# Attention's end in a hybrid backbone: the sixth head's norm in three groups, the last output products dealt differently, and a product and some low parts moved to VectorE

## The chip, the cores and the metric

One core of one Trainium2 chip runs the kernel. The metric is the device time of one execution in microseconds (us), and lower is better. Five engines work side by side, each on its own list of instructions in order: TensorE (PE, and PEld for its weight loads), VectorE (DVE), ScalarE (ACT), GpSimd (POOL) and SyncE (SP), whose list issues the DMAs. Semaphores make one engine wait for another.

## The reference

Two layers run over 1024 latent tokens and 256 context tokens of width 1024. The first layer mixes tokens by differential attention, the second by an S5 state-space layer; each is followed by a squared-ReLU MLP, and each sublayer has an RMS norm before and after it with a modulated scale, shift and gate. What the change touches is the end of the first mixer and the step from it to the MLP:

```
def attend(q, k, v):
    s = jnp.einsum('bqhcd,bkhcd->bhcqk', q, k).astype(jnp.float32)
    p = jax.nn.softmax(s, axis=-1)
    w = p[:, :, 0] - lam * p[:, :, 1]
    o = jnp.einsum('bhqk,bkhe->bqhe', w.astype(v.dtype), v)
    return rmsnorm(o, subln_g) * (1.0 - lambda_init)
...
y_lat = jnp.einsum('bte,ed->btd', o_l, w_o)
...
x = x + g1 * rmsnorm(y_lat, norm_g[i, 1])
h = rmsnorm(x, norm_g[i, 2]) * (1.0 + s2) + sh2
x = x + g2 * rmsnorm(sqrelu_mlp(h, mlp_w1[i], mlp_w2[i]), norm_g[i, 3])
```

There are 8 heads, so o has 8 slices of 128 columns per token (counted 0 to 7 here), and each is normed by itself before the product with w_o.

## The kernel before

**Numbers.** Every large product is made of three matmuls on numbers cut in a high and a low part (`mm3`, lines 132 to 134): high by high, high by low, low by high. `split` (lines 137 and 138) makes the parts: ACT copies the high part, then DVE, or POOL where it is named, subtracts it from the source to give the low part. So each cut is an ACT instruction and then one on DVE or POOL that waits for it.

**Attention** (`phase_b`) is written out by hand: inside `manual()` all engines but SP take their instructions in the order of the code. A step n handles unit u of head h (n = 9 h + u, 72 of them, then five closing steps 72 to 76). Unit 0 is the context's two query tiles, units 1 to 8 are one tile of 128 queries each. In a step PE makes the scores of its unit; DVE reads them out of PSUM with their maxima (line 592), ACT takes the two exponentials (602), DVE combines them (610 to 613). PE transposes the weights of the unit before in three parts (625): w0 (four 128-wide transposes), w1 (two) and w2 (four). w0 and w1 or w2 leave PSUM either directly (`w_direct`: ACT 631, then DVE 632) or through a copy (`w_copy`: ACT 638 and 641, then POOL 642). Every second step PE multiplies the weights by the values (`values`), and ACT takes the pair's output out of PSUM (732) and squares it (735); a later step has PE sum the squares (`pair_sums`, 740) into two PSUM columns.

PE's waits in a step are filled with products dealt to three places, `fill(0)` to `fill(2)`. From n = 63 on these are products of heads 0 to 5 with the left half of w_o for one token tile (`wo_group`, at the steps of `wo_at`); the tuple `a` says how many of the four or six products go to each place. Their sum leaves by ACT (858) and a DMA to `wod`. Heads 6 and 7 are added at the end: `wo_last` in steps 74 and 75 for tiles 8, 9 and 0 to 4, and in `phase_c` for tiles 5 to 7.

Head 6's norm happens while head 7 runs. For a pair of query tiles `load6` brings its output and its factors from DRAM in two buffers each, and `norm6` multiplies them on POOL (796) and splits the result, with the low part on POOL, into oT[..][:, 6]. At n = 69 and 70 two pairs each are loaded at the step's start and normed at its end, at n = 71 the fifth. Head 7's norm (`norm7`) is a step behind its sums: POOL writes a diagonal matrix (144, 811), PE multiplies it by ones so that the factors lie along columns (815), DVE applies them (817) and `split` cuts.

**The next stage** (`phase_c`, and `second_group` and `mlp0_head` behind it) is not ordered by hand: a scheduler sets each engine's order from the code. DVE adds head 6 and 7's part to the sum read back from DRAM (1486); then the right half of w_o is multiplied in the groups g = 2 (context, tiles 8 and 9), 0 (tiles 0 to 3) and 1 (tiles 4 to 7). For each tile `finish` runs a chain: ACT squares both halves with their sums (1438, 1439), DVE multiplies the right half by the gate row G (1440, reads PSUM), POOL multiplies the left half a by G (1443) and makes the factor (1441, 144), DVE scales and adds x (1447), ACT and POOL take the second norm (149, 150, 144), ACT scales (1454). When a group's tiles are done, `feature` (`to_feature`) turns them over: per k of 8, PE transposes (333) into one of two PSUM banks, DVE (338, even k) or ACT (336, odd k) applies scale and shift into one of two buffers, and `split` cuts the result, the low part on POOL for groups 2 and 0. The MLP's first products for the context and for group 0 (written H,RT in the views) follow on PE between these transposes.

Of the kernel before, what the change touches and what calls it, by code (L numbers as in the profile page):

```python
# [10 lines left out]
ALU = mybir.AluOpType  # L11
# [59 lines left out]
class Prog:  # L71
# [610 lines left out]
    def phase_b(self):  # L682
# [24 lines left out]
        pb = self.bank(6)  # L707
# [29 lines left out]
        def pair_sums(h, pair):  # L737
            b = pb[:, 0:2] if pair == 4 or h == 7 and pair > 2 else self.PS[:, 1790:1792]
            for i in range(2):
                mm(b[:, i : i + 1], sq[:, 128 * i : 128 * i + 128], self.ones, start=True, stop=True)  # L740
            nc.scalar.activation(hst[:, 1, h, 2 * pair : 2 * pair + 2], b, AF.Copy)
# [43 lines left out]
        buf6 = [(nob, nrb), (self.wv(6, 256), self.wv(7, 256))]  # L785
        pairs6 = {6: (0, 1), 7: (2, 3), 8: (4,)}

        def load6(u):
            for (ob, rb), pair in zip(buf6, pairs6[u]):
                self.dma(ob, self.od[6, :, 256 * pair : 256 * pair + 256])  # L790
                self.dma(rb, self.rsd[6, 2 * pair : 2 * pair + 2].rearrange("a b -> (a b)").partition_broadcast(128))

        def norm6(u):
            for (ob, rb), pair in zip(buf6, pairs6[u]):
                g, c0 = cols7[pair]
                nc.gpsimd.tensor_tensor(ob, ob, rb, ALU.mult)
                self.split(self.oT[g][0][:, 6, c0 : c0 + 256], self.oT[g][1][:, 6, c0 : c0 + 256], ob, nc.gpsimd)
# [90 lines left out]
        with self.manual():  # L888
            for n in range(72 + 5):
# [6 lines left out]
                if front and n - 6 >= 9 and (n - 6) % 9 < 5 and (n - 6) // 9 < 7:  # L896
                    norm_load((n - 6) // 9 - 1, (n - 6) % 9)
                if h == 7 and u > 5:
                    load6(u)
                if front:  # L900
# [16 lines left out]
                if groups:  # L917
                    if n < 63 or 0 < u < 3:
                        a = self.FILLS.get(u, (0, 1, 5, 8))
                    else:  # L920
                        a = (0, 4, 4, 4) if u == 0 else (0, 2, 5, 6) if late else (0, 2, 4, 6)
                    if n > 71:
                        a = (0, 2, 4, 6) if n == 72 else (0, 4, 6, 6)
                    fills = [groups[0][0][a[i] : a[i + 1]] for i in range(3)]
# [159 lines left out]
                if h == 7:  # L1084
                    beside7(u)
                    if u > 5:
                        norm6(u)
                if tail and tail[0][0] == n:
# [327 lines left out]
    def phase_c(self):  # L1416
# [13 lines left out]
        def finish(g, i, y):  # L1430
# [4 lines left out]
            def s0():  # L1435
                self.tile_dma(x0, i, x)
                st = self.stat.next()
                nc.scalar.activation(b, y, AF.Square, scale=1.0 / 32, accum_out=st[:, 1:2])
                nc.scalar.activation(b, a, AF.Square, scale=1.0 / 32, accum_out=st[:, 0:1])
                nc.vector.tensor_tensor(b, y, G[m][:, 512:1024], ALU.mult)  # L1440
                nc.gpsimd.tensor_scalar(st[:, 0:1], st[:, 0:1], st[:, 1:2], EPS, ALU.add, ALU.add)
                self.rsqrt(st[:, 2:3], st[:, 0:1])
                nc.gpsimd.tensor_tensor(a, a, G[m][:, 0:512], ALU.mult)
                r[0] = st[:, 2:3]
# [13 lines left out]
        def feature(g, k, tmps=tmps):  # L1458
            m = 1 if g == 2 else 0
            return self.to_feature([t[i] for i in self.G_TILES[g]], A[:, m], B[:, m], self.hT[g][0], self.hT[g][1],  # L1460
                                   tb, tmps, k, nc.vector if g == 1 and k % 2 else None, k % 2 == 1)

# [5 lines left out]
        for nb in range(2):  # L1468
            wt = [] if nb else [None] * 6
            for kk in range(0 if nb else 3, 4):  # L1470
                raw, hi, lo = raws.pop(0) if raws else self.wo_load(kk, nb), wr.next(), wr.next()
                for j in range(2):
                    self.split(hi[:, j], lo[:, j], raw[:, j])
                    wt.append((hi[:, j], lo[:, j]))
# [1204 lines left out]
```

## Time and profile before

| what | value |
|---|---|
| median of 3 runs | 2810.94 us |
| lowest and highest of them | 2810.39 and 2814.80 us |
| the profiled execution's own time | 2805.7 us |
| its span, first to last instruction | 2803.9 us |
| TensorE clock granted, mean of the span | 0.994 |
| PE / PEld / DVE busy | 2702.6 / 2251.9 / 2000.8 us |
| ACT / POOL busy | 1420.8 / 900.0 us |

Busy times are sums over the span. In a row of the timeline stand the start, the time from start to end, the engine, the line, what is written and read, how many instructions were merged, and in brackets how long the engine sat idle before and what ended that. A row of the windows gives a stretch, its length, the busy time of PE, PEld, DVE, ACT and POOL with their instruction counts, the clock granted to TensorE as a share of full speed, the share of the DMA engines that was busy, and GB/s. A PE matmul of 512 columns shows 0.39 us from start to end, but the next one starts 0.23 us after it, so PE's own lost time is better read from the starts and from the idle time of PEld, whose load begins each matmul.

### The profile page before, as it was taken

The numbers are of one execution on the slowest core, as the hardware profiler recorded it, in microseconds if no ns is written. First come the engines' busy times: TensorE is split into PE (matmuls) and PEld (weight loads), VectorE is DVE, ScalarE is ACT, GpSimd is POOL, SyncE is SP. The second block draws the span as 40 slices with busy tenths as digits, with TensorE's granted clock in tenths as the row PEclk, the third lists the DMA queues.
The fourth block names the chain that finished last, engine by engine and source line by source line (L and its number), as shares of the span: only waits on it lengthen the run. The fifth ranks groups of instructions, "written<-read, shape, count | busy, mean of one in ns | idle before, by whom it ended". The sixth has DMA issues, their size and how long they took to land. (4 is left out here: it accounts for less than half of the span.)

```text
span 2803.9 us, 43710 instructions
## 1 busy us (share of the span) xinstructions
PE 2702.6 (96%) x15645; PEld 2251.9 (80%) x15645; DVE 2000.8 (71%) x2994; ACT 1420.8 (51%) x2717; POOL 900.0 (32%) x729
## 2 busy tenths in 40 slices
PE   6999999999999999999999999799999999999999
PEld 4687888888777888888877788788787778888887
DVE  6366888888744777666898876899433687767566
ACT  3425677777655643333444444587344533345443
POOL 3312345554445400000120032687023053335414
PEclk9999999999999999999999999899999999999999
DMA  9944133333526378985899875689642254476544
GB/s 269 324 165 158 59 95 94 96 97 115 190 65 199 113 256 287 322 294 180 309 311 300 273 233 201 218 242 310 210 143 91 68 186 157 151 259 212 170 128 143
DMA packets 377448, 539.13 MB, mean 192 GB/s; under 512 B 38286, under 2 KB 231052, under 8 KB 374028
## 3 DMA queue, kind: packets, MB, share of 16 engines
q1 hardware_dynamic: 377228, 536.32, 58.6%
q8 instruction: 123, 2.02, 0.3%
q14 instruction: 97, 0.79, 0.1%
HBM read 367.54 MB, written 164.47 MB: 190 GB/s over the span
## 5 line engine op out<-in xcount | busy, mean ns | idle before, releaser
L132 PE MATMUL PS<-H 128*128 128x512 f32 x1072 | 420.5, 393 | 2.5 <-ACT H L137 1.4
L134 PE MATMUL PS<-H 128*128 128x512 f32 x1072 | 417.6, 390 | 3.2 <-DVE H L138 1.8
L133 PE MATMUL PS<-H 128*128 128x512 f32 x1072 | 417.7, 390 | 0.0
L132 PE MATMUL PS<-H,R 128*128 128x512 f32 (+1 forms) x828 | 307.8, 374 | 4.0 <-ACT R L137 1.5
L134 PE MATMUL PS<-H,R 128*128 128x512 f32 (+1 forms) x828 | 297.8, 360 | 0.9 <-POOL R L138 0.9
L133 PE MATMUL PS<-H,R 128*128 128x512 f32 (+1 forms) x828 | 298.1, 360 | 0.0
L132 PEld LDWEIGHTS PS<-H 128*128 128x128 f32 x1072 | 201.2, 188 | 50.4 <-issue 6.2
L134 PEld LDWEIGHTS PS<-H 128*128 128x128 f32 x1072 | 201.2, 188 | 46.6 <-DVE H L138 3.1
L133 PEld LDWEIGHTS PS<-H 128*128 128x128 f32 x1072 | 201.3, 188 | 40.6
L137 ACT ACTIVATE H<-U 128x640 fp32r<-128x640 f32 x216 | 131.9, 674 | 171.9 <-PE PS L133 143.9
L137 ACT ACTIVATE R<-W 128x512 fp32r<-128x512 f32 (+1 forms) x185 | 129.6, 707 | 171.4 <-PE PS L133 113.5
L132 PE MATMUL PS<-R,H 128*128 128x512 f32 x534 | 212.9, 400 | 3.2 <-ACT H L137 3.2
L134 PE MATMUL PS<-R,H 128*128 128x512 f32 x534 | 210.5, 395 | 1.8 <-DVE H L138 1.8
L133 PE MATMUL PS<-R,H 128*128 128x512 f32 x534 | 209.5, 393 | 0.0
L602 ACT ACTIVATE F<-F,stat 128x1280 f32<-128x1280 f32 x128 | 174.1, 1361 | 64.3 <-DVE F L592 64.3
L138 DVE TENSOR_TENSOR H<-U,H 128x640 fp32r<-128x640 f32 x216 | 167.0, 807 | 48.7 <-ACT H L137 45.5
L137 ACT ACTIVATE H<-W 128x512 fp32r<-128x512 f32 (+2 forms) x158 | 95.6, 614 | 198.4 <-PE PS L133 113.9
L138 DVE TENSOR_TENSOR H<-W,H 128x512 fp32r<-128x512 f32 (+1 forms) x137 | 125.9, 929 | 96.4 <-ACT H L137 95.9
L592 DVE TENSOR_SCALAR_CACHE_REDUCE F<-PS 128x1280 f32<-128x1280 f32 x128 | 185.3, 1485 | 13.0 <-PE PS L579 12.6
L642 POOL TENSOR_TENSOR R<-F,R 128x512 fp32r<-128x512 f32 (+1 forms) x88 | 119.3, 1367 | 209.9 <-ACT R L641 144.9
L132 PEld LDWEIGHTS PS<-H,R 128*128 128x128 f32 x828 | 156.9, 190 | 33.4 <-issue 4.1
L134 PEld LDWEIGHTS PS<-H,R 128*128 128x128 f32 x828 | 156.7, 189 | 26.4 <-POOL R L138 1.1
(529 smaller groups left out, 6688.4 us busy)
## 6 DMA issues: line engine op xcount, KB each, us to landing
W<-in_mlp_w SPq DMA_DIRECT2D x176, 256.0 KB, 3.7
U<-Aa SPq DMA_DIRECT2D x108, 320.0 KB, 4.4
Aa<-FU SPq DMA_DIRECT2D x91, 320.0 KB, 4.8
Ad<-F SPq DMA_DIRECT2D x112, 256.0 KB, 3.0
W<-Ad SPq DMA_DIRECT2D x112, 256.0 KB, 2.9
FU<-in_mlp_w SPq DMA_DIRECT2D x32, 512.0 KB, 5.9
Ta<-FU SPq DMA_DIRECT2D x16, 1024.0 KB
U<-in_ada_w SPq DMA_DIRECT2D x32, 512.0 KB, 9.1
```

The source lines that it names most:

```text
L132: mm(out, ah, bh, start=first, stop=False, **kw)
L133: mm(out, ah, bl, start=False, stop=False, **kw)
L134: mm(out, al, bh, start=False, stop=last, **kw)
L137: self.nc.scalar.activation(hi, src, AF.Copy)
L138: (lo_eng or self.nc.vector).tensor_tensor(lo, src, hi.bitcast(F32), ALU.subtract)
L592: ts(p[c], self.PS[:, 1792 * c : 1792 * c + 1280], 1.0, None, ALU.mult, ALU.min, accum_out=sm[:, c : c + 1])
L602: nc.scalar.activation(p[c], p[c], AF.Exp, bias=sm[:, c : c + 1], scale=-1.0, accum_out=sn[:, 0:1] if c else s0[:, u + 1 : u + 2])
L642: self.nc.gpsimd.tensor_tensor(lo, t, hi.bitcast(F32), ALU.subtract)
```

## The change

Six edits. (1) Head 6's norm runs in three groups, a step apart each: products on POOL (`norm6`) at the ends of steps 69, 71 and 73, the splits (`halves6`) at the ends of 70, 72 and 74; the next group's loads follow the splits. (2) At n = 63 one product moves from `fill(0)` to `fill(2)`; in the late steps 69 and 71 one moves from `fill(2)` to `fill(1)`. (3) The sums of head 7's last two pairs go to PSUM bank 5 in place of bank 6, which also holds the transposed weights and the last values. (4) a*G goes from POOL to DVE. (5) Group 0's low parts go from POOL to DVE. (6) One low part of w_o's last rows goes from DVE to POOL.

```
-            b = pb[:, 0:2] if pair == 4 or h == 7 and pair > 2 else self.PS[:, 1790:1792]
+            b = self.bank(5)[:, 0:2] if h == 7 and pair > 2 else pb[:, 0:2] if pair == 4 else self.PS[:, 1790:1792]
...
-        def norm6(u):
-            for (ob, rb), pair in zip(buf6, pairs6[u]):
+        def norm6(j):
+            for ob, rb in buf6[: len(pairs6[j])]:
+                nc.gpsimd.tensor_tensor(ob, ob, rb, ALU.mult)
+
+        def halves6(j):
+            for (ob, rb), pair in zip(buf6, pairs6[j]):
                 g, c0 = cols7[pair]
-                nc.gpsimd.tensor_tensor(ob, ob, rb, ALU.mult)
                 self.split(self.oT[g][0][:, 6, c0 : c0 + 256], self.oT[g][1][:, 6, c0 : c0 + 256], ob, nc.gpsimd)
...
-                if h == 7 and u > 5:
-                    load6(u)
+                if n == 69:
+                    load6(0)
...
-                        a = (0, 4, 4, 4) if u == 0 else (0, 2, 5, 6) if late else (0, 2, 4, 6)
+                        a = (0, 3, 3, 4) if u == 0 else (0, 2, 6, 6) if late else (0, 2, 4, 6)
...
-                    if u > 5:
-                        norm6(u)
+                if n in (69, 71, 73):
+                    norm6((n - 69) // 2)
+                if n in (70, 72, 74):
+                    halves6((n - 70) // 2)
+                    if n < 74:
+                        load6((n - 68) // 2)
...
-                nc.gpsimd.tensor_tensor(a, a, G[m][:, 0:512], ALU.mult)
+                nc.vector.tensor_tensor(a, a, G[m][:, 0:512], ALU.mult)
...
-                                   tb, tmps, k, nc.vector if g == 1 and k % 2 else None, k % 2 == 1)
+                                   tb, tmps, k, nc.vector if g == 0 or g == 1 and k % 2 else None, k % 2 == 1)
...
-                    self.split(hi[:, j], lo[:, j], raw[:, j])
+                    self.split(hi[:, j], lo[:, j], raw[:, j], None if nb or j else nc.gpsimd)
```

The lines of the new kernel stand 3 to 7 higher: 811 is 814 there, 815 is 818, 858 is 861, 1440 is 1447, 1443 is 1450, 1447 is 1454.

ACT's order before, from the end of step 69 to the exponentials of step 71 (H<-W is head 6's high part, FC head 7's output, 631 step 70's w0):

```order
L858 ACTIVATE W<-PS 128x512
L137 ACTIVATE H<-W 128x256 x2
L631 ACTIVATE R_110<-PS 128x4x128
L602 ACTIVATE F_1851,FC<-F_1851,stat 128x1280
L602 ACTIVATE F_1851,stat<-F_1851,stat 128x1280
L638 ACTIVATE F_1851<-PS 128x512
L631 ACTIVATE R_110<-PS 128x2x128
L641 ACTIVATE R_110<-F_1851 128x4x128
L741 ACTIVATE FC<-PS 128x2
L858 ACTIVATE W<-PS 128x512
L137 ACTIVATE H<-FC 128x256
L137 ACTIVATE H<-W 128x256 x2
```

And the same stretch now:

```order
L861 ACTIVATE W<-PS 128x512
L631 ACTIVATE R_110<-PS 128x4x128
L602 ACTIVATE F_1851,FC<-F_1851,stat 128x1280
L602 ACTIVATE F_1851,stat<-F_1851,stat 128x1280
L638 ACTIVATE F_1851<-PS 128x512
L631 ACTIVATE R_110<-PS 128x2x128
L641 ACTIVATE R_110<-F_1851 128x4x128
L741 ACTIVATE FC<-PS 128x2
L861 ACTIVATE W<-PS 128x512
L137 ACTIVATE H<-FC 128x256
L137 ACTIVATE H<-W 128x256 x2
```

The first two copies of head 6 have left the place ahead of step 70's w0; those that stand at the end of step 70 are now of the first group, whose products POOL made a step earlier.

POOL's order now, over the same steps and on to the diagonals of step 73 (795 is head 6's product, R_110<-W the split of w_o's last rows, 814 a diagonal):

```order
L795 TENSOR_TENSOR W<-W 128x256 x2
L642 TENSOR_TENSOR R_110<-F_1851,R_110 128x4x128
L138 TENSOR_TENSOR H<-FC,H 128x256
L138 TENSOR_TENSOR R_110<-W,R_110 128x1024
L138 TENSOR_TENSOR H<-W,H 128x256 x2
L144 TENSOR_TENSOR FC<-FC,mhalf 128x2
L814 TENSOR_SCALAR FC<-ident,FC 128x128 x2
```

These rows begin at the end of step 71: two products stand there where one product and its low part stood, and two low parts now stand between the split of w_o and the diagonal that PE waits for in step 73.

DVE's order before, for the chains of tiles 5 and 6 and the first features of group 0 (FA<-PS,FB is the right half by G, 1447 the scaling with x added, 338 a feature's scale and shift):

```order
L1440 TENSOR_TENSOR FA<-PS,FB 128x512
L1447 SCALAR_TENSOR_TENSOR W<-FA,stat,W 128x1024
L338 TENSOR_SCALAR FA<-PS,modc 128x512
L1440 TENSOR_TENSOR FA<-PS,FB 128x512
L1447 SCALAR_TENSOR_TENSOR W<-FA,stat,W 128x1024
L338 TENSOR_SCALAR FA<-PS,modc 128x512
```

And now:

```order
L1447 TENSOR_TENSOR FA<-PS,FB 128x512
L1450 TENSOR_TENSOR FA<-FA,FB 128x512
L1454 SCALAR_TENSOR_TENSOR W<-FA,stat,W 128x1024
L338 TENSOR_SCALAR FA<-PS,modc 128x512
L1447 TENSOR_TENSOR FA<-PS,FB 128x512
L1450 TENSOR_TENSOR FA<-FA,FB 128x512
L1454 SCALAR_TENSOR_TENSOR W<-FA,stat,W 128x1024
L138 TENSOR_TENSOR H<-FA,H 128x512 x2
L338 TENSOR_SCALAR FA<-PS,modc 128x512
L138 TENSOR_TENSOR H<-FA,H 128x512
```

A product (1450) has come between each tile's 1447 and its scaling, and group 0's low parts (138, H<-FA) stand between the features' 338. Over the program DVE has 17 instructions more (10 products, 8 low parts, one low part less) and POOL 17 fewer; all differences of order lie between step 63 and the MLP's first products.

More of the change, by code (lines that the diff above doesn't have):

```diff
@@ L785, in phase_b, with load6 @@
         buf6 = [(nob, nrb), (self.wv(6, 256), self.wv(7, 256))]
-        pairs6 = {6: (0, 1), 7: (2, 3), 8: (4,)}
-        def load6(u):
-            for (ob, rb), pair in zip(buf6, pairs6[u]):
+        pairs6 = (0, 1), (2, 3), (4,)
+        def load6(j):
+            for (ob, rb), pair in zip(buf6, pairs6[j]):
                 self.dma(ob, self.od[6, :, 256 * pair : 256 * pair + 256])
                 self.dma(rb, self.rsd[6, 2 * pair : 2 * pair + 2].rearrange("a b -> (a b)").partition_broadcast(128))
-        def norm6(u):
-            for (ob, rb), pair in zip(buf6, pairs6[u]):
+        def norm6(j):
+            for ob, rb in buf6[: len(pairs6[j])]:
+                nc.gpsimd.tensor_tensor(ob, ob, rb, ALU.mult)
+        def halves6(j):
+            for (ob, rb), pair in zip(buf6, pairs6[j]):
                 g, c0 = cols7[pair]
-                nc.gpsimd.tensor_tensor(ob, ob, rb, ALU.mult)
                 self.split(self.oT[g][0][:, 6, c0 : c0 + 256], self.oT[g][1][:, 6, c0 : c0 + 256], ob, nc.gpsimd)
```

## Prediction

> **What bounds the kernel now.** I read the page first:
>
> ```profile
> span 2803.9 us, 43710 instructions
> PE 2702.6 (96%) x15645; PEld 2251.9 (80%) x15645; DVE 2000.8 (71%) x2994; ACT 1420.8 (51%) x2717; POOL 900.0 (32%) x729
> ```
>
> TensorE is busy 96% of the span, so a change of order can only win back what TensorE loses. Two windows, both far behind the edited stretch, show what follows it:
>
> ```profile
> 1050.00:1100.00 50.00, 50.00 (x270) 39.98 (x270) 37.03 (x60) 17.36 (x34) 0.00 (x0) 1.00 0.89 307
> 1770.00:1775.00 5.00, 0.37 (x2) 0.37 (x2) 4.14 (x4) 3.47 (x7) 1.72 (x5) 0.66 1.05 340
> ```
>
> In the MLP TensorE has no gap at all (50.00 of 50), so an earlier start there is an earlier end; at 1770, in the S5 stage, it stands still (0.37 of 5) while the DMA engines are full. Then I took the edited stretch, 735 to 945 us, and listed what TensorE's loads waited for. First how a wait is read, from the end of step 72:
>
> ```profile
> 822.69 0.39 PE L133 MATMUL PS<-R,H 128*128 128x512 f32 x1
> 822.92 0.40 PE L134 MATMUL PS<-R,H 128*128 128x512 f32 x1
> 823.94 0.52 PEld L740 LDWEIGHTS PS<-lamc,adat 128*128 128x128 f32 x4 [1.05 <-DVE R L632]
> ```
>
> Matmuls start 0.23 apart, so the one at 822.92 held TensorE until 823.15, and the sums of squares started at 823.94: 0.79 was lost where the load shows 1.05 idle. About 0.26 of such an idle time is no loss, and I take it off below.
>
> The largest wait of the attention's end is in step 70, with the rows of all engines in order of time:
>
> ```profile
> 797.90 0.60 PE L625 MATMUL PS<-ident,F 128*128 128x128 f32 x4
> 798.01 1.49 DVE L592 TENSOR_SCALAR_CACHE_REDUCE F<-PS 128x1280 f32<-128x1280 f32 x1
> 798.71 0.42 ACT L137 ACTIVATE H<-W 128x256 fp32r<-128x256 f32 x1 [3.09 <-POOL W L796]
> 799.21 0.74 POOL L138 TENSOR_TENSOR H<-W,H 128x256 fp32r<-128x256 f32 x1 [0.53 <-ACT H L137]
> 800.67 0.42 ACT L137 ACTIVATE H<-W 128x256 fp32r<-128x256 f32 x1 [1.53 <-POOL W L796]
> 800.99 0.58 ACT L631 ACTIVATE R<-PS 128x512 fp32r<-128x512 f32 x1
> 801.60 0.69 DVE L632 TENSOR_TENSOR R<-PS,R 128x512 fp32r<-128x512 f32 x1 [2.10 <-ACT R L631]
> 802.35 0.20 PEld L625 LDWEIGHTS PS<-ident,F 128*128 128x128 f32 x2 [2.28 <-DVE R L632]
> 804.79 0.52 PEld L740 LDWEIGHTS PS<-lamc,adat 128*128 128x128 f32 x4 [1.03 <-ACT F L638]
> ```
>
> w0's transposes end at 798.50, but ACT sits in front of head 6's first high part until POOL's product is there (3.09), then of the second (1.53), and copies w0 only at 800.99. VectorE's low part follows at 801.60 and w1's transposes, which need its bank, at 802.35: TensorE waited 2.28. The other waits, of steps 63, 71 and 74:
>
> ```profile
> 738.36 0.52 PEld L740 LDWEIGHTS PS<-lamc,adat 128*128 128x128 f32 x4 [1.52 <-ACT F L638]
> 816.71 0.42 PEld L625 LDWEIGHTS PS<-ident,F 128*128 128x128 f32 x4 [1.36 <-DVE R L632]
> 833.77 0.52 PEld L740 LDWEIGHTS PS<-lamc,adat 128*128 128x128 f32 x4 [0.91 <-DVE FC L817]
> ```
>
> and behind them those before the last rows of w_o and in the next stage, with the clock there:
>
> ```profile
> 846.67 0.53 PEld L132 LDWEIGHTS PS<-RT,H 128*128 128x128 f32 x3 [1.20 <-ACT RT L137]
> 848.06 3.69 DVE L138 TENSOR_TENSOR RT<-W,RT 128x512 fp32r<-128x512 f32 x6
> 848.80 0.19 PEld L133 LDWEIGHTS PS<-RT,H 128*128 128x128 f32 x1 [1.60 <-DVE RT L138]
> ```
>
> ```profile
> 874.72 0.20 PEld L333 LDWEIGHTS PS<-ident,FB 128*128 128x128 f32 x2 [0.86 <-ACT FB L1454]
> 884.71 0.20 PEld L333 LDWEIGHTS PS<-ident,FB 128*128 128x128 f32 x2 [0.53 <-DVE FA L338]
> 890.63 0.20 PEld L333 LDWEIGHTS PS<-ident,FB 128*128 128x128 f32 x2 [1.11 <-ACT FA L336]
> 913.68 0.42 PEld L333 LDWEIGHTS PS<-ident,FB 128*128 128x128 f32 x4 [2.74 <-DVE FA L338]
> 915.42 0.71 PEld L333 LDWEIGHTS PS<-ident,FB 128*128 128x128 f32 x4 [0.58 <-ACT FA L336]
> 920.40 0.42 PEld L333 LDWEIGHTS PS<-ident,FB 128*128 128x128 f32 x4 [1.24 <-DVE FA L338]
> ```
>
> ```profile
> 910.00:915.00 5.00, 2.68 (x15) 1.85 (x13) 2.27 (x3) 2.94 (x8) 2.33 (x4) 0.98 0.58 207
> 915.00:920.00 5.00, 4.28 (x23) 3.73 (x21) 3.10 (x3) 2.80 (x5) 4.82 (x6) 0.68 0.37 106
> ```
>
> The features' transposes wait for the banks that VectorE (338) and ScalarE (336) empty, and behind the longest gap, 2.74, the granted clock falls to 0.68 for a window.
>
> **The change part by part.** *Step 63.* One product leaves the place ahead of w0, so w0 and all behind it come its 0.68 (3 x 0.23) earlier, and it runs again inside the 1.52 that TensorE waited for the copy of w2. Gain 0.68; the cover is the 1.52, and were it gone the gain would be nil.
>
> *Step 70.* The product-and-split pairs become two products alone, with the ACT copies a step later. ACT is then free when w0 is there. What is late next is VectorE: its second maxima end at 798.01 + 1.49 = 799.50, so the low part moves from 801.60 to 799.50, and w1's transposes, 0.75 behind it, to 800.25, where TensorE arrives anyway. The sums at 804.79 hang on ACT's two exponentials and copy behind w0; ACT starts these about 2.4 earlier (798.60 for 800.99), so I take 2.4 for the step, 2.0 at the least (2.28 less 0.26), 3.0 at most (with all of the 1.03).
>
> *Step 71.* The ACT copies at its start no longer wait for POOL, and a fourth product fills the place ahead of w2's transposes. That wait was 1.36, a loss of 1.1; filled by 0.68 and shortened by the earlier ACT, I take all of it: 1.1 (0.7 by the product alone).
>
> *Steps 72 and 74.* In bank 5 the sums wait neither for w0's low part nor for head 7's multiplication (817), which were the releasers: 0.79 and 0.91 - 0.26 = 0.65. Both go unless the next matmul then waits (below). The DMAs of head 6 are issued later, behind the splits of the group before; no product to DRAM is held by them for longer than before, since the waiting buffer is free one POOL instruction after ACT's copy. Attention's end together: 0.68 + 2.4 + 1.1 + 0.79 + 0.65 = 5.6.
>
> *Last rows of w_o.* The first low part goes to POOL, which is idle there, in 1.29 (the row of a 128x512 low part below); on VectorE it stood behind the sums that wait for DRAM, until 848.06. ACT's high part is there when the first matmul that reads it starts, 846.67, so the low part ends by 847.9 in place of 848.06 + 0.62 = 848.7: 0.8 of the 1.60. Bounds nil and 1.34.
>
> *The product a*G.* The chain of one tile before:
>
> ```profile
> 909.31 0.69 DVE L1440 TENSOR_TENSOR FA<-PS,FB 128x512 f32<-128x512 f32 x1 [2.55 <-ACT FA L1439]
> 909.76 1.30 POOL L1443 TENSOR_TENSOR FA<-FA,FB 128x512 f32<-128x512 f32 x1
> 911.01 0.58 POOL L144 TENSOR_TENSOR stat<-stat,mhalf 128x1 f32<-128x1 f32 x1
> 911.62 1.28 DVE L1447 SCALAR_TENSOR_TENSOR W<-FA,stat,W 128x1024 f32<-128x1024 f32 x1 [1.62 <-POOL stat L144]
> 912.83 0.81 DVE L338 TENSOR_SCALAR FA<-PS,modc 128x512 f32<-128x512 f32 x1
> ```
>
> POOL's product (1.30) stands between the sum's first step and the root at 911.01, which releases the scaling at 911.62 and so the feature at 912.83. Without it the root comes 1.25 earlier; on VectorE the same product takes about 0.69 (the 1440 row, the same shape from PSUM) in the time in which VectorE waits for the root (1.62). So each of ten chains becomes some 1.25 shorter, and 0.69 is hidden in the wait that remains.
>
> *Group 0's low parts.* Eight of them leave POOL and go to VectorE:
>
> ```profile
> 921.98 1.29 POOL L138 TENSOR_TENSOR H<-FA,H 128x512 fp32r<-128x512 f32 x1 [0.26 <-ACT H L137]
> 935.52 1.67 DVE L1512 TENSOR_TENSOR FA<-FA,H 128x512 f32<-128x512 f32 x1
> ```
>
> At 921.98 one took 1.29 on POOL. On VectorE a low part of this shape takes 3.69 / 6 = 0.62 when it runs alone (the row at 848.06), and an operation with the same shape and both inputs in SBUF took 1.67 at 935.52, when POOL ran a low part beside it. These are the bounds, 8 x 0.62 = 5.0 and 8 x 1.67 = 13.4; POOL is left with little but roots in this stretch, so I take the lower end, and add the delay it makes where it stands between features.
>
> The Trainium skill's SBUF page (SBUF — State Buffer, "Who interferes with whom") says that a VectorE instruction with two SBUF inputs and a GpSimd instruction that reads SBUF exclude each other for a whole instruction; the 1.67 here agrees. By that rule the moved work gains only where POOL is quiet.
>
> What TensorE gets of it: the waits at 874.72, 884.71 and 890.63 (0.86 + 0.53 + 1.11, less 3 x 0.26 = 1.7) are chains of groups 2 and 0, each shorter by more than its wait; I take 1.7. The next, 2.74 and 0.58, end at tile 5's chain, in front of which tile 4's stands in the same queues: two times 1.25 cover 2.48 (2.74 - 0.26), and the 0.58 is the odd feature behind the same. The 1.24 at 920.40 stands behind tile 6's chain, and here two low parts now stand in VectorE's order ahead of the feature. I take 2.74 + 0.58 + 1.24 - 0.78 = 3.8 less 1.0 that stays, 2.8; bounds 0 and 3.8. And the clock: 5 x 0.32 + 5 x 0.02 = 1.7 us of work lost in the two windows. It fell right behind the 2.74 and not behind the 2.28 of step 70, so with that gap gone I count all 1.7.
>
> The Trainium skill's page TensorE: Matmul & The Clock Gate ("What's actually happening") lets the clock fall only after an idle window of about 3.4 us, longer than this gap; by that rule the gap was not the cause, the 1.7 would stay, and the gain would be 1.7 smaller. The trace here shows the fall behind 2.74, and I go by it.
>
> Sum: 5.6 + 0.8 + 1.7 + 2.8 + 1.7 = 12.6 us. The profiled execution took 2805.7 (span 2803.9) and would take 2793.1; it lies 5.2 below the median of the runs, 2810.94, from which I take the same 12.6: 2798.3.
>
> **The rivals.** *The rest does not follow.* TensorE comes 12.6 earlier into an MLP where the DMA engines are 0.89 busy, and into the S5 stage, where TensorE stands while they are full. If the loads there keep their own time, the gain is swallowed: 2810.9. Against it: TensorE shows no wait on a load in the MLP, and the loads are issued as their buffers come free, so earlier too.
>
> *POOL becomes late in step 73.* There head 7's factors need POOL's diagonal:
>
> ```profile
> 830.18 0.72 POOL L811 TENSOR_SCALAR FC<-ident,FC 128x128 f32<-128x128 f32 x2
> 832.67 0.59 PE L815 MATMUL PS<-FC 128*128 128x256 f32 x2
> ```
>
> It was done at 830.90, 1.77 ahead of its reader. The new order puts two low parts (0.74 each, as at 799.21) in front, and TensorE comes about 5 earlier. If POOL moved up not at all, TensorE would wait 5 - 1.77 + 1.48 = 4.7; its own inputs come earlier too, so I expect some tenths. With 4.7 lost the gain is 7.9: 2803.0.
>
> *VectorE becomes the bound (slower).* It gets 17 instructions, 17 x 0.69 = 11.7 us, or 17 x 1.67 = 28.4 at the price beside POOL. Group 0's low parts wait for ACT inside VectorE's ordered list, and behind them wait the scalings of tiles 6 and 7 and the next features, whose banks TensorE waits for. If each of eight comes at 1.67 with 0.5 of waiting, 17.4 land on the path and the two waits that follow cost another 1.7 of clock each: 20.8 - 5.6 - 0.8 = 14.4 slower, 2825.3. It decides the sign once more than 6.4 us land there in place of the 6.2 gained. For it: the ordering; against it: the 1.62 of waiting in each chain and POOL's silence.
>
> **How the numbers follow.** Forecast 0.62, no carry-over 0.14, POOL late 0.12, VectorE the bound 0.12. Runs of this kernel can be told apart at about 0.2%, 5.6 us. The forecast's own bounds: all waits of the list and the clock, 5.6 + 0.6 + 1.34 + 1.7 + 3.8 + 1.7 = 14.7, with 4 us for the spread of the runs (2810.39 to 2814.80) down to 2791; the low ends, 0.7 + 2.0 + 0.7 + 0 + 1.0, give about 4.4, 2806.5. The range 2791 to 2807 holds the forecast and POOL's case. Faster by over 0.2%: 0.75 (0.62 and 0.12, and a little for the rest); within 0.2%: 0.15; slower: 0.10.
>
> **What would show it.** Right: head 6's high parts at steps 70 and 71 with no wait on POOL; w1's transposes of step 70 right behind w2's; no load idle over 0.5 at the sums of steps 72 and 74; no idle load over 1.5 among the features and a clock of 1.00 throughout 860 to 940; the MLP's first full window earlier by about 12. Wrong: a wait of step 73's factors on POOL's diagonal; loads that wait on VectorE's low parts of group 0 for more than a microsecond; or the stretch shorter and the S5 stage later against the MLP's end by the same amount.

## The result and the profile after

The changed kernel takes 2791.78 us (median of 6 runs, 2788.81 to 2796.62) where the kernel before took 2810.66 beside it (2809.36 to 2814.80): a ratio of 0.9933, 95% interval 0.9920 to 0.9946, or 18.9 us (15.2 to 22.5). On another occasion the same two kernels stood at 0.9948 (0.9936 to 0.9959), 14.6 us (11.5 to 18.0). The forecast was 12.6.

```profile
span 2793.9 us, 43702 instructions
PE 2697.4 (97%) x15645; PEld 2249.3 (81%) x15645; DVE 2002.0 (72%) x3011; ACT 1419.8 (51%) x2717; POOL 875.3 (31%) x712
```

The profiled execution took 2795.67, so it shows only 10.0 us against that of before. To see which part of this belongs to the change, I read three marks in each trace, the same instructions every time. Here they are in the kernel before: the maxima ahead of step 63, the last factors of head 7, and the S5 stage's first transposes, which follow the MLP's last matmul.

```profile
726.23 1.48 DVE L592 TENSOR_SCALAR_CACHE_REDUCE F<-PS 128x1280 f32<-128x1280 f32 x1
...
839.81 0.59 PE L815 MATMUL PS<-FC 128*128 128x256 f32 x2
...
1766.77 0.50 PE L1908 MATMUL PS<-ident 128*128 128x128 f32 x3
```

And after, first in the trace that came with the result, then in a second execution of the same kernel:

```profile
726.97 1.48 DVE L592 TENSOR_SCALAR_CACHE_REDUCE F<-PS 128x1280 f32<-128x1280 f32 x1
...
834.21 0.59 PE L818 MATMUL PS<-FC 128*128 128x256 f32 x2
...
1755.50 1.06 PE L1915 MATMUL PS<-ident 128*128 128x128 f32 x8
```

```profile
725.54 1.48 DVE L592 TENSOR_SCALAR_CACHE_REDUCE F<-PS 128x1280 f32<-128x1280 f32 x1
...
832.82 0.59 PE L818 MATMUL PS<-FC 128*128 128x256 f32 x2
...
1750.30 1.06 PE L1915 MATMUL PS<-ident 128*128 128x128 f32 x8
```

From the first mark to the second, attention's end, it is 113.58 before, and 107.24 and 107.28 after: 6.3 us gained both times. From the second to the third, the next stage with the MLP, it is 926.96 before, and 921.29 and 917.48 after: 5.7 and 9.5 gained. So the whole edited stretch gained 12.0 in the one trace and 15.8 in the other. What lies outside it is the same code in both kernels, and it varies: from the start to the first mark 726.2, 727.0 and 725.5, from the third to the end of the span 1037.1, 1038.4 and 1039.8.

The step with the largest wait, step 70, in the changed kernel:

```profile
797.63 0.60 PE L625 MATMUL PS<-ident,F 128*128 128x128 f32 x4
797.75 1.49 DVE L592 TENSOR_SCALAR_CACHE_REDUCE F<-PS 128x1280 f32<-128x1280 f32 x1
798.27 0.60 ACT L631 ACTIVATE R<-PS 128x512 fp32r<-128x512 f32 x1 [2.21 <-PE PS L625]
799.16 0.69 DVE L632 TENSOR_TENSOR R<-PS,R 128x512 fp32r<-128x512 f32 x1
799.90 0.20 PEld L625 LDWEIGHTS PS<-ident,F 128*128 128x128 f32 x2
802.09 0.52 PEld L740 LDWEIGHTS PS<-lamc,adat 128*128 128x128 f32 x4 [0.78 <-ACT F L638]
```

ACT now waits for TensorE (2.21), not for POOL; the low part follows the maxima directly, and w1's transposes are loaded at 799.90 with no idle time (2.28 before). In the rows below the sums of steps 72 and 74 (the first two) show none either. In step 73 POOL's two low parts now stand ahead of the diagonals, which are done at 827.55, 0.31 ahead of the factors that need them; before it was 1.77:

```profile
819.04 0.65 PEld L740 LDWEIGHTS PS<-lamc,adat 128*128 128x128 f32 x4
828.08 0.63 PEld L740 LDWEIGHTS PS<-lamc,adat 128*128 128x128 f32 x4
824.61 1.44 POOL L138 TENSOR_TENSOR H<-W,H 128x256 fp32r<-128x256 f32 x2
826.82 0.73 POOL L814 TENSOR_SCALAR FC<-ident,FC 128x128 f32<-128x128 f32 x2
827.86 0.59 PE L818 MATMUL PS<-FC 128*128 128x256 f32 x2
```

At w_o's last rows the wait did not go. In the same trace:

```profile
841.09 1.29 POOL L138 TENSOR_TENSOR RT<-W,RT 128x512 fp32r<-128x512 f32 x1 [2.46 <-ACT RT L137]
844.99 0.69 DVE L1493 TENSOR_TENSOR FA<-FA,PS 128x512 f32<-128x512 f32 x1 [4.57 <-DMA FA<-wod]
845.59 2.49 DVE L138 TENSOR_TENSOR RT<-W,RT 128x512 fp32r<-128x512 f32 x4
846.33 0.50 PE L133 MATMUL PS<-RT,H 128*128 128x512 f32 x1 [1.57 <-DVE RT L138]
```

POOL has the first low part done at 842.38. TensorE goes on with it, and stands 1.57 for the second, which VectorE makes behind a sum that waited 4.57 for its load from DRAM.

Last, the windows that were slowest in the next stage before:

```profile
910.00:915.00 5.00, 5.00 (x27) 4.22 (x27) 3.57 (x5) 4.68 (x11) 0.86 (x2) 1.00 0.30 90
915.00:920.00 5.00, 5.00 (x39) 4.68 (x38) 3.18 (x6) 4.45 (x8) 0.74 (x2) 1.00 0.27 108
```

TensorE is busy throughout, at full clock, and the two windows show 66 matmuls where they showed 38.

### The profile page after: what moved, and what is told of

Same layout as the page of the kernel before. It is cut to its first block, busy times and chain, and to the rows that moved or that the text cites. A ratio compares the mean times of both kernels' runs of the same rounds, so it can differ in the third digit from the quotient of the medians.

```text
span 2793.9 us, 43702 instructions
## 1 busy us (share of the span) xinstructions
PE 2697.4 (97%) x15645; PEld 2249.3 (81%) x15645; DVE 2002.0 (72%) x3011; ACT 1419.8 (51%) x2717; POOL 875.3 (31%) x712
## 4 chain that ended last, share of the span: by engine, by line
PE 53%; DVE 6%; DMA 4%; issue 2%; POOL 1%; ACT 1%; SPq 0%; DVEq 0%; POOLq 0%; ACTq 0%
PE PS L132 16%; PE PS L134 16%; PE PS L133 16%; PE PS L2035 2%; PE PS L2070 1%; DVE H L138 1%; DMA W<-in_mlp_w 1%; DVE R L138 1%; DMA FU<-in_mlp_w 1%; DVE FD L2053 1%; DVE FD L2044 1%; PE PS L1344 1%; PE PS L202 0%; PE PS L1350 0%; DMA K<-in_mlp_w 0%
```

## The experiments

**The theories.** A is the sum as forecast. B says that the end agrees but the parts do not: part of attention's gain is lost at w_o's last rows, where TensorE meets loads that come no earlier, the first low part on POOL gives nothing, and the next stage gains more than forecast.

All traces by the three marks, in us. "Falls" are the times in the stretch at which the granted clock fell to a half; of each kernel but the changed one and the one with both low parts on POOL there is one trace.

| kernel | 1 to 2 | 2 to 3 | falls |
|---|---|---|---|
| before | 113.58 | 926.96 | 915 |
| changed | 107.24 | 921.29 | none |
| changed, again | 107.28 | 917.48 | none |
| edits 1 to 3 alone | 108.57 | 927.39 | 740, 917 |
| edits 4 and 5 alone | 116.35 | 918.15 | 737 |
| without edit 6 | 107.22 | 917.40 | none |
| both low parts on POOL | 107.67 | 916.76 | none |
| the same, again | 107.24 | 919.13 | none |
| a*G on POOL | 107.27 | 926.13 | none |
| group 0's low parts on POOL | 107.30 | 920.76 | 848 |
| without bank 5 | 108.05 | 919.31 | none |
| without the new dealing | 109.87 | 916.30 | 736 |
| edit 1 alone | 110.72 | 927.42 | 742, 851, 919 |
| a second instruction behind a*G | 108.57 | 922.32 | 735 |

**Edits 1 to 3 alone** (the changed kernel with these lines as before):

```
-                nc.vector.tensor_tensor(a, a, G[m][:, 0:512], ALU.mult)
+                nc.gpsimd.tensor_tensor(a, a, G[m][:, 0:512], ALU.mult)
...
-                                   tb, tmps, k, nc.vector if g == 0 or g == 1 and k % 2 else None, k % 2 == 1)
+                                   tb, tmps, k, nc.vector if g == 1 and k % 2 else None, k % 2 == 1)
...
-                    self.split(hi[:, j], lo[:, j], raw[:, j], None if nb or j else nc.gpsimd)
+                    self.split(hi[:, j], lo[:, j], raw[:, j])
```

> The kernel before with edits 1 to 3 alone (head 6's norm in three groups, the dealing of the fills, bank 5); a*G, group 0's low parts and the first low part of w_o's last rows stay where they were. Theory A, the forecast's own sum: the 5.6 us of attention's end reach the end, about 2805. Theory B, read from the two traces: TensorE comes 5.6 earlier at the last factors, but the loads of the sums in DRAM, in front of VectorE's low part for w_o's last rows, come only 2.5 earlier, so some 3 of the 5.6 are lost there and about 2.5 remain: about 2808. By B TensorE's first load of the second low part shows an idle time longer than the 1.60 of before; by A it doesn't.

Measured: ratio 0.998 (0.997 to 0.999), 5.6 us (2.8 to 8.4). In the trace attention's end gained 5.0 although the clock fell in step 63; the next stage took 0.4 longer than before, with 1.05 us of TensorE idle in the MLP (298.95 busy of the 300 from 950 to 1250). TensorE did stand for the second low part, 1.36 for 1.17 before, but that is 0.2 longer and not 3. So A holds and B's first half falls: I had compared the time of that wait in two traces, and ahead of it the new kernel had done more matmuls than the old one.

**Edits 4 and 5 alone** (the kernel before with these):

```
-                nc.gpsimd.tensor_tensor(a, a, G[m][:, 0:512], ALU.mult)
+                nc.vector.tensor_tensor(a, a, G[m][:, 0:512], ALU.mult)
...
-                                   tb, tmps, k, nc.vector if g == 1 and k % 2 else None, k % 2 == 1)
+                                   tb, tmps, k, nc.vector if g == 0 or g == 1 and k % 2 else None, k % 2 == 1)
```

> The kernel before with edits 4 and 5 alone (a*G and group 0's low parts on VectorE). Theory A, the forecast's sum: 1.7 of waits before 900 us, 2.8 of the three waits behind 913 us and 1.7 of clock, 6.2 in all, about 2804.5. Theory B, read from the traces: between the first w_o product and the MLP the change gained about 10 us, so 9 to 10 here, about 2801. By the rival that VectorE becomes the bound it would be slower than before. Both theories expect a granted clock of 1.00 in every window of 860 to 945 us; if the clock still falls there although no gap of over 1.5 us stands in front, the gap of 2.74 was not its cause.

Measured: 0.9967 (0.9955 to 0.9979), 9.3 us (5.9 to 12.6), and 8.8 in the trace between marks 2 and 3. B's second half holds in the trace: the next stage gives more than 6.2; the interval of the times reaches down to 5.9. The clock was 1.00 from 860 to 945. The two halves, 5.6 and 9.3, make 14.9. The whole change gave 14.6 when its second trace was taken, and 18.9 (15.2 to 22.5) at first; the halves do not account for the 4 more of that first comparison.

**Without edit 6** (the last two lines of the first diff):

> The changed kernel without edit 6: the first low part of w_o's last rows is back on VectorE. Theory A (forecast): 0.8 us slower than the changed kernel, about 2792.6. Theory B: no difference (within 0.5), since in the changed kernel TensorE gets past the first low part only to wait for the second, which stands on VectorE behind the same sum that waits for DRAM; the wait moves, and its end does not.

Measured: 0.9942 (0.9929 to 0.9955), between the changed kernel's 0.9933 and 0.9948. The times can't show 0.8 us; in the trace the next stage took 917.40, no more than the changed kernel's 921.29 and 917.48, as B says. TensorE stood 0.79 at the second low part.

**Both low parts on POOL:**

```
-                    self.split(hi[:, j], lo[:, j], raw[:, j], None if nb or j else nc.gpsimd)
+                    self.split(hi[:, j], lo[:, j], raw[:, j], None if nb else nc.gpsimd)
```

> The changed kernel with both low parts of w_o's last rows on POOL. Theory B: the second low part is then ready at about 843.7 us instead of 846.2, TensorE's wait of 1.57 for it goes, and the kernel is 1.5 to 2 us faster than the changed one, about 2790. Rival C: TensorE meets the same load a little later, because the sums' PSUM banks or the next low parts are late by as much; then no difference (within 0.5).

Measured: 0.9943 (0.9930 to 0.9957). The stop is gone, the load of the next low part on VectorE shows 0.15:

```profile
843.56 0.69 DVE L1493 TENSOR_TENSOR FA<-FA,PS 128x512 f32<-128x512 f32 x1 [3.49 <-DMA FA<-wod]
844.16 2.49 DVE L138 TENSOR_TENSOR RT<-W,RT 128x512 fp32r<-128x512 f32 x4
844.90 0.19 PEld L133 LDWEIGHTS PS<-RT,H 128*128 128x128 f32 x1 [0.15 <-DVE RT L138]
```

But the time is the changed kernel's within the interval, so an effect of 1.5 us on it is neither shown nor excluded.

**The changed kernel again:**

> The changed kernel once more, for its profile and its times beside the other runs. The medians so far gave it 18.9 us and the one traced execution only 10.0. Measured on the edited stretch alone (from the first scores after step 62 to the MLP's end) the first trace had gained 12.0, 13.7 without a gap of 1.67 in the MLP, where TensorE waited for a vector of the next layer that stood on VectorE behind a load. Theory A: that gap belongs to the single execution, so it is not here, and the edited stretch gains 13 to 14. Theory B: the gap belongs to the changed kernel (its VectorE order and its earlier loads) and stands here too, with 12.

Measured: 2791.91 us (2790.15 to 2797.57, 5 runs), ratio 0.9948; the stretch gained 15.8. A holds as far as the gap goes: there was none between 950 and 1300. The first trace had it here:

```profile
1257.57 0.69 DVE L1679 TENSOR_TENSOR FU<-FU 128x512 f32<-128x512 f32 x1 [1.77 <-DMA FU<-in_mlp_w]
1258.18 0.17 DVE L233 TENSOR_TENSOR modc<-modc,ng 128x16 f32<-128x16 f32 x1
1258.40 0.13 PEld L291 LDWEIGHTS PS<-ident,modc 128*96 128x96 f32 x1 [2.09 <-DVE modc L233]
```

VectorE waited 1.77 for a load and did the modulation vector only after it; TensorE's transpose of that vector waited for both. The gap came back in one other trace, the second one of the kernel with both low parts on POOL (48.27 busy of the 50 from 1250 to 1300). It is a matter of when the load lands. The gain of 13 to 14 that A named was too small: TensorE stood 0.30 in place of 1.57 at w_o's last rows, and was busy for 90.00 of the 90 us from 860 to 950, where the first trace had 89.48.

**a*G back on POOL** (the first two lines of the first diff):

> The changed kernel with a*G back on POOL; group 0's low parts stay on VectorE. Theory A, the forecast's reading: a*G makes each chain 1.25 shorter and carries nearly all of the next stage's gain, so the waits behind the features return and the stretch from head 7's last factors to the MLP's end is 6 us longer than in the changed kernel. Theory B: the eight low parts had kept POOL from the roots of the chains too, so their leaving is worth about half; then 3 to 5 us longer. In both the granted clock falls again behind the group's last chains only if a gap over 2 us is back.

Measured: 0.9968 (0.9956 to 0.9980) beside 0.9948 of the changed kernel, 5.6 us slower at the middle; between marks 2 and 3 it took 926.13, 4.8 and 8.7 longer than the two traces of the changed kernel. Those two differ by the gap in the MLP (1.67) and by their stops at w_o's rows (1.57 and 0.30, here 1.70); with these taken off it is 6.4 and 7.2. That speaks for A: in the trace nearly the whole gain of the next stage is gone without the moved product, and the stop behind the group's last chains is back:

```profile
915.51 0.66 PE L333 MATMUL PS<-ident,FB 128*128 128x128 f32 x4 [2.85 <-DVE FA L338]
```

What I had not expected: the clock stayed at 1.00 behind it. (Why these windows are 3.41 long is told below, with the clock.)

```profile
910.75:914.16 3.41, 1.92 (x16) 1.71 (x15) 3.41 (x5) 1.15 (x2) 3.16 (x5) 1.00 0.38 156
914.16:917.58 3.42, 2.07 (x14) 1.94 (x15) 1.30 (x2) 2.40 (x4) 1.10 (x2) 1.00 0.39 157
917.58:920.99 3.41, 3.17 (x16) 2.29 (x16) 2.10 (x3) 3.41 (x8) 1.70 (x4) 1.00 0.53 152
```

**Group 0's low parts back on POOL** (lines three and four of the first diff):

> The changed kernel with group 0's low parts back on POOL; a*G stays on VectorE. Theory A, the forecast's reading: these eight moves gain nothing and cost up to 1.0 where they stand on VectorE between features, so this kernel is the same or up to 1 us faster. Theory B: POOL was busy 4.6 to 4.8 of 5 us between 890 and 930, so the roots and these low parts queue there, and 2 to 4 us of the next stage's gain are lost again, with waits of TensorE on POOL's low parts or on the features.

Measured: 0.9944 (0.9932 to 0.9955), not to be told from the changed kernel, and 920.76 between the marks. Of the 3.3 above the changed kernel's second trace a fall of the clock is 1.7, and a longer stop at w_o's rows, ahead of these low parts, 1.5 (1.85 for 0.30). That leaves A: no gain of these eight moves shows. TensorE showed no wait on them on either engine.

**Without bank 5:**

```
-            b = self.bank(5)[:, 0:2] if h == 7 and pair > 2 else pb[:, 0:2] if pair == 4 else self.PS[:, 1790:1792]
+            b = pb[:, 0:2] if pair == 4 or h == 7 and pair > 2 else self.PS[:, 1790:1792]
```

> The changed kernel with the sums of head 7's last two pairs back in bank 6. The forecast: 0.79 at step 72 and 0.65 at step 74 come back, so the stretch from step 63 to the last factors is 1.4 us longer than the changed kernel's 107.24. Rival: the sums' wait had moved to the next matmul anyway, or the earlier copies of w0 now free bank 6 in time, and it is longer by less than 0.4.

Measured: 108.05, 0.8 longer, and 2794.53 in its one run. Of the two waits one came back, step 74's, whole (0.51 on TensorE, as in the kernel before):

```profile
828.12 0.42 DVE L820 TENSOR_TENSOR FC<-FC,PS 128x256 f32<-128x256 f32 x1 [7.04 <-PE PS L818]
828.60 0.61 PE L740 MATMUL PS<-lamc,adat 128*128 128x1 f32 x4 [0.51 <-DVE FC L820]
```

Step 72's did not: the stretch from the factors at 802.17 to those at 819.27 took 17.10, as in the changed kernel (802.55 to 819.64, 17.09). So neither answer was right as a whole; bank 5 is worth 0.8 in place of 1.44.

**Without the new dealing:**

```
-                        a = (0, 3, 3, 4) if u == 0 else (0, 2, 6, 6) if late else (0, 2, 4, 6)
+                        a = (0, 4, 4, 4) if u == 0 else (0, 2, 5, 6) if late else (0, 2, 4, 6)
```

> The changed kernel with the dealing of before (edit 2 undone). The forecast gave it 0.68 at step 63 and 0.7 of step 71's 1.1, so the stretch from the scores before step 63 to the last factors is 1.4 longer than the changed kernel's 107.24 to 107.30: 108.6 to 108.7. Rival: in step 71 the earlier ACT copies alone bring the low part in time, so only the 0.68 of step 63 come back: 107.9.

Measured: 109.87, with a fall of the clock in step 63, and 2787.71 in its one run. Behind that fall two steps are longer than in the changed kernel: from the maxima at 783.79 to those at 794.96 it took 11.17 for 10.87, and from the factors at 801.18 to those at 818.66 17.48 for 17.09. That is 0.30 in step 69 and 0.39 in steps 71 and 72. Together they are the 0.7 of the forecast, which had put all of it in step 71 and nothing in step 69; step 63's own 0.68 can't be told from the clock's loss here.

**Edit 1 alone** (the changed kernel with the lines of the two diffs just shown, and of the first one, as before):

> The kernel before with edit 1 alone (head 6's norm in three groups). The forecast: 2.4 at step 70 and 0.4 of step 71, 2.8 in all, and the same stretch takes 113.58 - 2.8 = 110.8. Rival: since the wait of step 72's sums did not return when bank 6 was given back, that 0.79 belongs to this edit too, and the stretch takes 110.0 or less. If the granted clock falls behind one of its gaps, the stretch is longer by the clock's loss, and the steps are read one by one.

Measured: 110.72 with a fall in step 63, where it took 15.62 to the next step's maxima for 14.85 before, and 11.28 for 10.78 in the step behind; without these 1.3 it is 109.4, and 2807.25 in its one run. Read step by step: step 70, from the maxima at 799.99 to those at 809.81, took 9.82 where before it took 12.26 (796.59 to 808.85), so 2.44; from the factors at 806.21 to those at 823.69, 17.48 for 19.14, so 1.66. The rival was right: the sums of step 72 show no wait in this trace, so it goes with this edit alone, 4.1 in all.

**A second instruction behind a*G:**

```
-                nc.vector.tensor_tensor(a, a, G[m][:, 0:512], ALU.mult)
+                nc.vector.tensor_tensor(a, a, G[m][:, 0:512], ALU.mult); nc.vector.tensor_tensor(a, a, a, ALU.max)
```

> The changed kernel with a second VectorE instruction of the same shape behind each of the ten a*G (the maximum of a with itself, so the values stay); the scheduler places the rest anew. It doubles the cost that the forecast hid in the wait for the root. Theory A: half a microsecond more in each chain is still covered, TensorE shows no idle load over 0.6 among the features, and the stretch from the last factors to the MLP's end is within 1 us of the changed kernel's 917.5. Rival, VectorE the bound: with a*G in place of POOL's root it is already VectorE that ends the chain, so 10 x 0.69 come back as waits at the features, 3 to 7 us.

Measured: 0.9957 (0.9941 to 0.9972), not to be told from the changed kernel by the times; in the trace 922.32 between marks 2 and 3, 4.8 above the 917.5, though only 1.0 above the changed kernel's first trace, which has the gap in the MLP and the longer stop at w_o's rows. Stops behind VectorE are back: 0.93 and 1.66 at features, and 0.78 at a low part of the MLP's weights, 3.4 together. The largest:

```profile
905.49 0.69 DVE L1450 TENSOR_TENSOR FA<-FA 128x512 f32<-128x512 f32 x1
906.09 0.69 DVE L138 TENSOR_TENSOR H<-FA,H 128x512 fp32r<-128x512 f32 x1
906.69 1.28 DVE L1454 SCALAR_TENSOR_TENSOR W<-FA,stat,W 128x1024 f32<-128x1024 f32 x1
907.89 0.81 DVE L338 TENSOR_SCALAR FA<-PS,modc 128x512 f32<-128x512 f32 x1
908.75 0.66 PE L333 MATMUL PS<-ident,FB 128*128 128x128 f32 x4 [1.66 <-DVE FA L338]
```

Added work, a low part, scaling and feature stand on VectorE back to back, and TensorE waits for the last. By the trace the rival is borne out: the changed kernel has no room on VectorE for another 0.69 in each chain. How much that costs rests on this one trace.

**Both low parts on POOL, again:**

> The changed kernel with both low parts of w_o's last rows on POOL, once more. In eight traces TensorE stood 0 to 2.3 us at a low part of these rows that VectorE makes behind the sums from DRAM, with the first low part on POOL (five traces, 1.5 in the mean) as without (1.0 to 1.4); in the one trace with both on POOL it did not stand. Theory B: the wait is the second low part's, and is gone here again, under 0.3; the kernel is as fast as the changed one or up to 1.5 us faster. Rival: the first time was luck of the DMAs, and a wait over 1 us stands here too.

(The traces meant there are nine, and without edit 6 the stops were 0.8 to 1.4.) Measured: 0.9936 (0.9924 to 0.9948); TensorE stood 0.46, and lost 1.73 to the gap in the MLP. With the later traces the stops at the second low part are: with the first on POOL 1.57, 0.30, 1.70, 1.85, 2.29, none and 0.57, in the mean 1.2; with both on VectorE 1.17, 1.36, 1.04, 0.79 and 2.69, 1.4; with both on POOL none and 0.46. Edit 6 alone does not shorten them measurably. With both on POOL they are about a microsecond shorter in the mean, but two traces do not show it for sure, since others had none, 0.30 and 0.57 too; neither answer was met by the 0.46. The times (0.9943, 0.9936) can't be told from the changed kernel's.

## Why the prediction was right

By the marks the stretch gained 12.0 and 15.8 where 12.6 was forecast; by the times it was 18.9 (15.2 to 22.5) and 14.6 (11.5 to 18.0). So the way was right and the sum rather too small, and that 2791.78 still lies inside 2791 to 2807, by 0.8, is in part luck.

**Attention's end: right, 6.3 for 5.6.** By the first trace, each mark counted from the first mark, the steps gained: step 63 0.66 (forecast 0.68); the steps behind it to 796.59 0.34 (not forecast; it is the late steps' dealing, which acts in step 69 too); step 70 2.44 (2.4); steps 71 and 72 2.06 (1.1 + 0.79), of which edit 1 alone gave 1.66 and the dealing 0.39; step 74 0.84 (0.65). The owner was wrong once: I gave step 72's 0.79 to bank 5, and edit 1 takes it away by itself. When one edit lets an engine come earlier, a wait behind it that the same engine released can go with it.

**The last rows of w_o: wrong.** The step "ACT's high part is there when the first matmul that reads it starts, 846.67, so the low part ends by 847.9 in place of 848.7: 0.8 of the 1.60" looked at one low part only. POOL did finish it early (842.38), but the next one has the same sum in front of it. What decides is the load, for which that sum waited 4.57. Between 835 and 845 the DMA engines are full now, where TensorE comes 5.6 earlier:

```profile
835.00:840.00 5.00, 5.00 (x24) 4.01 (x22) 3.20 (x6) 0.42 (x1) 0.74 (x1) 1.00 1.00 341
840.00:845.00 5.00, 3.90 (x15) 2.28 (x13) 0.43 (x2) 3.23 (x6) 1.29 (x1) 1.00 1.03 279
```

That the full DMA engines are why the load lands late is argued, and not shown. In the changed kernel's second execution they are as full (1.01 and 1.04), and the stop was 0.30; another order of the loads wasn't tried.

**The product a*G: the right cause, its chain by another amount.** One chain after:

```profile
901.12 0.69 DVE L1447 TENSOR_TENSOR FA<-PS,FB 128x512 f32<-128x512 f32 x1 [3.48 <-ACT FA L1446]
901.58 0.57 POOL L144 TENSOR_TENSOR stat<-stat,mhalf 128x1 f32<-128x1 f32 x1
901.73 0.68 DVE L1450 TENSOR_TENSOR FA<-FA,FB 128x512 f32<-128x512 f32 x1
902.50 1.28 DVE L1454 SCALAR_TENSOR_TENSOR W<-FA,stat,W 128x1024 f32<-128x1024 f32 x1
```

The root is done at 902.15, the product at 902.41, and the scaling follows at 902.50. So VectorE ends this chain now, and it is 1.38 from the start of the first product to the scaling where it was 2.31: 0.93 shorter, not 1.25. "0.69 is hidden in the wait that remains" was not quite so, since no wait remains. It was enough for all the stops: none was left between 860 and 950 in the second trace (90.00 busy of 90). What a*G is worth by itself, 5.6 in the times and 6.4 to 7.2 in the traces, is about the 1.7 + 2.8 + 1.7 of the forecast. That is partly luck: the clock did not fall in the trace with a*G on POOL, so its 1.7 is not in this difference, and the waits alone gave more than the 4.5 that the forecast had for them.

**Group 0's low parts: right.** They ran on VectorE in 0.68 to 0.69 each, near the lower end, between 907 and 922.5 of the first trace, and no low part of POOL stood beside them; they gain nothing that shows. Further on in that trace, at 928.15, a low part of the same shape ran beside one of POOL's and took 1.78. The Trainium skill's SBUF page (SBUF — State Buffer, "Who interferes with whom") has a VectorE instruction with two SBUF inputs contend with a GpSimd instruction that reads SBUF, and the two durations agree.

**What the forecast left out.** "3.8 less 1.0 that stays" was too careful, and my list ended at 920.40, though TensorE lost time in two more windows before:

```profile
925.00:930.00 5.00, 4.57 (x30) 3.95 (x30) 3.10 (x2) 3.65 (x9) 4.79 (x7) 1.00 0.26 103
940.00:945.00 5.00, 4.12 (x31) 3.71 (x30) 5.00 (x8) 4.93 (x10) 0.88 (x1) 1.00 0.33 111
```

The first was a wait for a low part of POOL, the second for one that VectorE made of the MLP's weights. With their 0.43 and 0.88, which are gone after, and the 1.0, the next stage's 7.0 less the 0.8 of w_o becomes 8.5; 8.8 were measured for edits 4 and 5.

**The clock: the loss right, the rule as I used it wrong.** I took the fall at 915 for the sure result of the 2.74 behind which it stood (2.32 on TensorE itself). Stops of that kind among the features (2.3 to 2.9 on TensorE) are in four traces; the clock fell behind three, and in the kernel with a*G on POOL it did not. And it fell behind much shorter ones. In the trace of edits 1 to 3, step 63:

```profile
736.94 0.44 PE L625 MATMUL PS<-ident,F 128*128 128x128 f32 x2 [0.98 <-DVE R L632]
738.65 0.61 PE L740 MATMUL PS<-lamc,adat 128*128 128x1 f32 x4 [0.58 <-ACT F L638]
```

```profile
736.18:739.59 3.41, 2.07 (x13) 1.54 (x15) 3.08 (x9) 3.41 (x12) 0.88 (x3) 1.00 1.02 330
739.59:743.00 3.41, 3.41 (x21) 2.72 (x18) 2.22 (x4) 1.32 (x3) 3.41 (x3) 0.50 0.26 86
```

Stops of 0.98 and 0.58 with work between them, and then a clock of 0.50 for 3.41 us: 1.7 us of work lost. The same pair stands in ten traces, and the clock fell in two; with the second stop at 1.28, as the kernel before has it, it fell in three of four.

What goes with a fall is how the stops lie. Within one execution all changes of the granted clock lie on one grid of 3.41 us, and this grid lies differently in each execution. The windows just shown are two of the grid. From the first mark to the third, in all traces, TensorE was busy for at most 0.46 of the window ahead of each of the ten falls, and for at least 0.45 of every window at full clock that no fall followed; the matmuls of line 740, which have one column, are left out of this. By this a stop counts by what it leaves of its window. That of the kernel before lies in one window, of which 1.13 or 0.33 was busy, and the clock fell at its end:

```profile
911.41:914.82 3.41, 1.13 (x7) 1.04 (x8) 2.09 (x3) 1.88 (x5) 0.74 (x3) 1.00 0.77 274
914.82:918.23 3.41, 3.33 (x15) 2.83 (x15) 1.51 (x2) 2.63 (x4) 3.23 (x5) 0.50 0.08 29
```

The 2.85 of the kernel with a*G on POOL was cut by the grid at 914.16, which left 0.56 and 0.61 busy (the windows shown there), and no fall came. So the 1.7 of my sum was the loss of the one execution I had, and another execution with the same stops may lose it or not; in the trace of edits 4 and 5 alone a fall lasted two windows.

The Trainium skill's page TensorE: Matmul & The Clock Gate ("What's actually happening") has the activity judged in a free-running window of about 3.4 us; the grid agrees, and so does it that the same stop falls differently from run to run. By the Trainium skill's table there the clock falls after an idle window; the windows ahead of the ten falls were busy for 0.24 to 0.61 of their time, line 740 counted, so a window needn't be idle throughout.

The kernel before has both kinds of stop, and its one trace showed one fall; runs with more would explain why the times show more than 12.6. The mean clocks of whole runs point that way: the traced run of the kernel before had 0.994, the 41 measured beside the experiments 0.989 to 0.994 with 0.991 in the middle. The changed kernel's traced runs had 0.993, and all its eleven 0.992 in the middle. Where in those runs the clock fell is not known.

**The rivals.** "The rest does not follow" fell: from the third mark to the end it was 1037.1 before and 1036.3 to 1040.1 in the others, with no trend. "POOL late" fell, but by a margin of 0.31 that had been 1.77: the two low parts came in front as feared, and from the first mark POOL was done 4.1 earlier all the same, where TensorE came 5.6 earlier. "VectorE the bound" fell for this change but was near, as the stops with the doubled product show.

## What to carry to other kernels

Before pricing what a faster engine gains at a wait, look at the next instruction of the same kind in the queue: if the same load stands in front of it, the wait only moves. Move an instruction off the engine that ends a chain, and check whether it now ends on the engine that received it; one more instruction there may already cost. To judge ten microseconds in a kernel of which equal code varies by several, cut the trace at the same instructions on both sides of the edit, and look at more than one execution.

## What the runs showed of the hardware

In the edited stretch the granted clock fell to a half for 3.41 us at a time, once for two such windows, on one grid within each execution; a fall of one window cost 1.7 us. It fell behind ten windows of the grid in which TensorE, the one-column matmuls aside, was busy for at most 0.46, and behind none in which it was busy for more. So stops as short as 0.98 and 0.58 in one window were followed by a fall, and one of 2.85, cut by the grid, was not. Code that is the same in all kernels took 723.2 to 728.7 us from the start to the first mark and 1036.3 to 1040.1 from the third to the end. One load that lands later, in front of an ordered VectorE list, cost 1.7 us of TensorE in the MLP in two of the traces and nothing in the changed kernel's second execution.
